# First block's output projection at 512 columns a product and tile by tile, and more points of giving way in the RWKV chain

## The chip, the core and the metric

The kernel runs on one core of one Trainium2 chip. The metric is the time of one execution on the device in microseconds, here the median of several runs; the trace is one execution taken by the hardware profiler. TensorE is PE in the rows (its weight loads PEld), VectorE is DVE, ScalarE ACT, GpSimd POOL; SP issues most of the DMA.

## The reference

Three blocks follow each other on one sequence of 1,024 tokens of width 1,024, in fp32. Cut to what the change touches:

```python
# first block: three mixers, gated and merged, then the output projection and a layer norm
log_om = where(causal, log_sigmoid(-z), 0)               # stick-breaking attention, blocks of 128 tokens
weights = masked_exp(causal, log_sigmoid(z) + reverse_cumsum(log_om) - log_om)
...
out = einsum('btd,de->bte', merged, w_out)               # 1024 x 1024 x 1024
x = layer_norm(DEEPNORM_ALPHA * x + out, ln_g, ln_b)

# second block: RMS norm, one wide projection, RWKV-7 time mix beside dilated attention
xn = rms_norm(h, norm_w)
p = einsum('bsd,dn->bsn', xn, w_in)
# time mix, per head of 64 and per token
sa = einsum('bhvk,bhk->bhv', state, av_t)
state = state * w_t + sa[..., None] * bv_t + v_t[..., None] * k_t
y_t = einsum('bhvk,bhk->bhv', state, r_t)
```

The third block follows and is not touched.

## The kernel before

Every fp32 operand of a dense product is split in a high and a low part (`split`: ACT casts the high part, DVE subtracts), and a product is three matmuls, high by high, high by low and low by high (`mm3`, L310 to L312). Dense products of the projections into a mixer keep 128 weight columns in the array and stream 512 tokens. Python generators write the program: `interleave` takes from each generator a count of expected steps and a start and an end in relative time, and always advances the one that is furthest behind by steps done over that count; each `yield` is a point where another may be written. What is written is then ordered by the scheduler of the recording layer for each engine; every engine executes its own instructions in that order.

*The mixes of the first block* (`mixing1`) run in six stages. In stage n the dense products of mixer n and some gates are interleaved with the mix of mixer n - 1. The stick-breaking mix (`stick`, stages two and three) goes over eight blocks of 128 tokens: products (L568), two sigmoids on ACT, masks and a reversed scan on DVE (L577), a multiply (L578), transposes on PE (L589), copies (L591) and products with the values (L597). `M1` gives `interleave` the count of its steps, 60, which is also how many there are.

*The output projection* is in `out1`. After the up projections (eight steps of L310 to L312 into `m`, twice) it holds the merged activations as `macts`, 128 x 512 in each of eight pieces for each half of the tokens. `wout(hf)` does one half of the tokens, four tiles of 128: for each quarter of 256 output columns `tok4_gen` streams the eight weight slices past the four tiles (L362 to L364, 256 columns a matmul) into two PSUM banks, and `ev` adds the residual x (L838) and takes statistics (L839). The x of a half is loaded ahead of it (L832). After the last quarter of a half `norms` finishes a tile: layer norm (L795 to L802; for the first `LNP` tiles one multiply on ACT and the addition on POOL, for the others one pass on DVE), the store of the result, and the RMS norm of the second block (`norm_act`, L860 to L862). `to_acts` transposes a normalized tile (L873) and splits it into `nacts`. The second half's products are interleaved with the transposes of the first half's tiles, and those of the second half with `rwkv_start`, four dense products of the second block on the first half of the tokens. Weights come through a pool of three raw buffers and five split ones.

*The RWKV time mix* (`rwkv`) has 16 units (pair of heads and half of the tokens), in 18 iterations. In iteration `it` it interleaves the chain of unit it - 2 (`rw_chain`), the inverse of unit it - 1 (`rw_inverse`, 62 small DVE passes), the features of unit it (`rw_feat`) and dense products (`rw_dense` and attention jobs). The chain has eight chunks of 64 tokens. Each is a line of dependent steps: products with the state (L1169), copies of the result into `R` on DVE and ACT (L1170, L1171), a product (L1174), copies into `SV` (L1175, L1176), a product (L1178), the new state on DVE (L1182) and a product into the output (L1183). A chunk has one `yield`, at its end. After the chunks the unit's output is normed (L1190 to L1197), transposed (L1204) and gated.

Of the kernel before, what the change touches and what calls it, by code (L numbers as in the profile page):

```python
# [10 lines left out]
F32R = mybir.dt.float32r  # L11
# [7 lines left out]
D = 1024  # L19
# [82 lines left out]
def layout(a):  # L102
# [41 lines left out]
    quarters = lambda w: f(w.reshape(-1, 128, w.shape[1] // 256, 256).transpose(2, 1, 0, 3))  # L144
    o["w1out"] = quarters(a["w_out"][0])
    o["w2out"] = quarters(a["w_out_2"])
# [4 lines left out]
    o["w3fm"] = tiles(w3, 8)  # L151
    halves = lambda w: f(w.reshape(-1, 128, w.shape[1] // 512, 512).transpose(2, 1, 0, 3))
    o["w3v"] = halves(w3[:, 512:1024])
# [27 lines left out]
MRB = 2  # L181
GNY = 4
TRM = (0.0, 0.8)
YD = 0
LNP = 4
HGD = 1
# [17 lines left out]
class Kern:  # L204
# [342 lines left out]
    def stick(self, pm, pr, q, k, v, y):  # L547

        nc = self.nc
        for i in range(NT):  # L550
# [10 lines left out]
            for h in range(2):  # L561
# [17 lines left out]
                bes.append(be)  # L579
                yield  # L580
            po = self.mm_ps()[:, :128]
            for g0 in range(0, i + 1, 4):
# [182 lines left out]
    def out1(self, acts):  # L765
# [4 lines left out]
        with self.weights(*WB[1]), tc.tile_pool(name="pu", bufs=1, reuse_waits="tile") as pu, self.psum(mx=4, tp=2):  # L770
# [22 lines left out]
            def norms(i, r, st):  # L793
                mv = self.t(pu, [128, 4], "lnmv", bufs=2)
                V.bn_aggr(mv[:, 0:2], st)  # L795
                self.rsqrt(pu, mv[:, 2:3], mv[:, 1:2], 1.0, 1e-5)
                V.scalar_tensor_tensor(r, r, mv[:, 0:1], g, ALU.subtract, ALU.mult)
                if i < LNP:
                    nc.scalar.activation(r, r, AF.Identity, scale=mv[:, 2:3])
                    nc.gpsimd.tensor_tensor(r, r, b, ALU.add)  # L800
                else:
                    V.scalar_tensor_tensor(r, r, mv[:, 2:3], b, ALU.mult, ALU.add)  # L802
                nc.scalar.dma_start(self.hd[i], r)
                return self.norm_act(pu, r, nw, 1e-5)

# [20 lines left out]

            def wout(hf):
                rs, sts = [], []
                for i in range(4):
                    rs.append(self.t(po, [128, D], "r", bufs=8))  # L830
                    sts.append(self.t(pu, [128, 4, 6], "lnst", bufs=8))
                    nc.sync.dma_start(rs[i], I["x"][512 * hf + 128 * i:512 * hf + 128 * i + 128])  # L832
                for q in range(4):

                    def ev(i, ps, q=q):
                        r, st = rs[i - 4 * hf], sts[i - 4 * hf]
                        qs = slice(256 * q, 256 * q + 256)
                        V.scalar_tensor_tensor(r[:, qs], r[:, qs], ALPHA, ps, ALU.mult, ALU.add)  # L838
                        V.bn_stats(st[:, q], r[:, qs])  # L839
                        if q == 3:  # L840
                            pend.append((i, norms(i, r, st)))
                    yield from self.tok4_gen(I["w1out"][q], macts, range(4 * hf, 4 * hf + 4), ev)

            def late():
                while pend:
                    self.to_acts(*pend.pop(0), nacts)
                    yield
            for _ in wout(0):
                pass
            interleave([(wout(1), 64, 0.0, 1.0), (late(), 4, 0.3, 0.9)])  # L850
            self.acts = nacts
            interleave([(self.rwkv_start(), 32, 0.0, 1.0), (late(), 4, 0.2, 1.1)])
            po_pool.__exit__(None, None, None)

    def norm_act(self, pool, h, nw, eps):

        nc = self.nc
        xs = self.t(pool, [128, D], "xs", bufs=2)
        ms = self.t(pool, [128, 2], "ms", bufs=2)
# [74 lines left out]
    def rwkv(self):  # L934
        nc, tc, I = self.nc, self.tc, self.I
        with tc.tile_pool(name="rw", bufs=1, reuse_waits="tile") as rw, self.psum(mx=2, iv=1, ch=1, cy=1):
# [15 lines left out]
            for it in range(18):  # L952
                gens = []
                if it >= 2:
                    gens.append((self.rw_chain(rw, U[it - 2]), 11 + GNY, *PLAN[0]))
                if 1 <= it <= 16:
                    gens.append((self.rw_inverse(rw, U[it - 1]), 37, *PLAN[1]))
                if it < 16:
                    gens.append((self.rw_feat(rw, U[it]), 20, *PLAN[2]))
                jobs = list(islice(att, ATT[it]))  # L960
# [22 lines left out]
    def rw_feat(self, rw, S):  # L983
# [20 lines left out]
        yield  # L1004
        V.tensor_tensor_scan(sg, self.c("cm"), sg, 0.0, ALU.mult, ALU.add)
        e1 = self.t(rw, [128, 8, 65], "E1")
        ei = ff("ei")
        nc.gpsimd.memset(e1[:, :, 0:1], 1.0)
        nc.scalar.activation(e1[:, :, 1:65], c8(sg), AF.Exp, scale=-cc)
        nc.scalar.activation(ei, sg, AF.Exp, scale=cc)  # L1010
        S["dc"] = dc = self.t(rw, [128, 8], "dc", bufs=3)
# [134 lines left out]
    def rw_chain(self, rw, S):  # L1146
# [16 lines left out]
        for c in range(8):  # L1163
# [8 lines left out]
            for n, s in enumerate((E, O)):  # L1172
                nc.scalar.activation(sd[s], sv[s, c, n], AF.Identity, scale=dc[s])  # L1173
            nc.tensor.matmul(up, xs[:, c], R, start=True, stop=True)  # L1174
            V.tensor_copy(sv[E, c, 0], up[E])  # L1175
            nc.scalar.copy(sv[O, c, 1], up[O])  # L1176
            both = sv[:, c].rearrange("p n v -> p (n v)")
            nc.tensor.matmul(sp, M3[:, c].rearrange("p n k -> p (n k)"), both, start=True, stop=True)  # L1178
            for n, s in enumerate((E, O)):
# [12 lines left out]
        TT(c8(y), c8(y), bc(st[:, 0:8]), ALU.add)  # L1192
        nc.scalar.activation(sq, y, AF.Square)
        yield
        V.tensor_reduce(st[:, 8:16], c8(sq), AX.X, ALU.add)
# [559 lines left out]
```

## Time and profile before

| | |
|---|---|
| median of 3 runs | 2845.41 us (2844.46 to 2849.97) |
| the profiled execution | 2842.42 us |
| its span | 2840.6 us |
| mean granted TensorE clock in it | 0.986 of full |
| busy: PE, PEld | 96%, 80% of the span |
| busy: DVE, ACT, POOL | 62%, 41%, 10% |

The span is the time from the first to the last instruction in the trace. The bars of matmuls overlap, so PE's busy share is how long it had something in work, not how much of its rate was used.

### The profile page before, as it was taken

How to read it: one execution, taken by the hardware profiler on the slowest of the kernel's cores; microseconds unless marked ns; L12 is line 12 of the kernel's file. 1: busy time of each engine (PE TensorE's matmuls, PEld its weight loads, DVE VectorE, ACT ScalarE, POOL GpSimd, SP SyncE). 2: the span in 40 equal slices, each digit the busy share in tenths (PEclk: the TensorE clock that was granted, in tenths of full speed). 3: DMA queues.
4: the chain of work that ended last, by engine and by line, in shares of the span. 5: the costliest groups of instructions: out<-in, count | busy, mean ns of one | idle time of the engine just before them, and what ended most of it. 6: DMA issues, size and time to landing. Idle time of an engine off the chain costs nothing. (4 is left out here: it accounts for less than half of the span.)

```text
span 2840.6 us, 50116 instructions
## 1 busy us (share of the span) xinstructions
PE 2732.7 (96%) x18984; PEld 2277.3 (80%) x18984; DVE 1762.3 (62%) x4655; ACT 1174.7 (41%) x2808; POOL 275.5 (10%) x370
## 2 busy tenths in 40 slices
PE   9999999999998999999999999989999999999999
PEld 7778787777798787778877778768889989978887
DVE  4665533433867567787787877765466676644354
ACT  4433323223324324444445444444465666442232
POOL 0000000000213100010011100100011211000100
PEclk9999999999999999999999999989999999999999
DMA  3121111114753322222222222222754553331132
GB/s 124 45 68 45 56 65 38 57 57 148 226 191 115 98 85 66 72 74 69 78 66 79 69 72 75 68 66 73 209 181 143 165 161 109 132 118 66 48 121 97
DMA packets 215265, 276.63 MB, mean 97 GB/s; under 512 B 70112, under 2 KB 105712, under 8 KB 214896
## 3 DMA queue, kind: packets, MB, share of 16 engines
q1 hardware_dynamic: 187024, 220.99, 25.4%
q10 hardware_dynamic: 28000, 52.44, 5.1%
q8 instruction: 149, 2.44, 0.4%
q14 instruction: 92, 0.75, 0.1%
HBM read 213.58 MB, written 59.77 MB: 96 GB/s over the span
## 5 line engine op out<-in xcount | busy, mean ns | idle before, releaser
L310 PE MATMUL pd<-aH,wh 128*128 128x512 f32 (+1 forms) x1824 | 758.5, 416 | 12.4 <-ACT aH L305 5.9
L312 PE MATMUL pd<-aH,wl 128*128 128x512 f32 (+1 forms) x1824 | 735.1, 403 | 2.2 <-DVE wl L282 2.2
L311 PE MATMUL pd<-aL,wh 128*128 128x512 f32 (+1 forms) x1824 | 731.2, 401 | 0.0
L282 DVE TENSOR_TENSOR wl<-wraw,wh 128x512 fp32r<-128x512 f32 (+1 forms) x429 | 305.0, 716 | 303.1 <-ACT wh L281 293.5
L281 ACT CAST wh<-wraw 128x512 fp32r<-128x512 f32 (+1 forms) x429 | 260.4, 611 | 433.8 <-PE pd L311 214.3
L310 PEld LDWEIGHTS pd<-aH,wh 128*128 128x128 f32 (+1 forms) x1824 | 345.8, 190 | 85.2 <-issue 14.4
L312 PEld LDWEIGHTS pd<-aH,wl 128*128 128x128 f32 (+1 forms) x1824 | 345.3, 189 | 72.6 <-DVE wl L282 4.5
L311 PEld LDWEIGHTS pd<-aL,wh 128*128 128x128 f32 (+1 forms) x1824 | 346.5, 190 | 57.9 <-DVE aL L306 0.4
L310 PE MATMUL pd<-wh,aH 128*128 128x256 f32 x960 | 283.1, 296 | 2.7 <-ACT wh L281 2.2
L311 PE MATMUL pd<-wl,aH 128*128 128x256 f32 x960 | 273.7, 286 | 0.9 <-DVE wl L282 0.9
L312 PE MATMUL pd<-wh,aL 128*128 128x256 f32 x960 | 272.1, 286 | 1.4 <-DVE aL L306 1.2
L310 PEld LDWEIGHTS pd<-wh,aH 128*128 128x128 f32 x960 | 183.4, 192 | 7.7 <-ACT wh L281 3.4
L311 PEld LDWEIGHTS pd<-wl,aH 128*128 128x128 f32 x960 | 183.8, 192 | 4.1 <-DVE wl L282 1.8
L312 PEld LDWEIGHTS pd<-wh,aL 128*128 128x128 f32 x960 | 183.3, 192 | 2.7 <-DVE aL L306 2.3
L1447 ACT ACTIVATE S<-S,anm 128x256 f32<-128x256 f32 (+1 forms) x256 | 118.0, 463 | 22.5 <-DVE anm L1440 19.5
L1173 ACT ACTIVATE sd<-SV,dc 64x64 f32<-64x64 f32 x256 | 88.4, 345 | 83.6 <-DVE SV L1182 78.4
L1111 DVE TENSOR_TENSOR Xt<-At,X 128x60 f32<-128x60 f32 (+24 forms) x496 | 106.4, 214 | 11.1
L1113 DVE TENSOR_TENSOR X<-X,Xt 128x60 f32<-128x60 f32 (+24 forms) x496 | 104.7, 211 | 12.2
L1398 DVE CUSTOM_DVE_ANT_0 S<-sc,cf 128x256 f32<-128x256 f32 (+1 forms) x256 | 86.1, 377 | 31.3 <-PE sc L1395 21.7
L1394 PE MATMUL sc<-kk,qq 128*128 128x256 f32 (+1 forms) x256 | 90.5, 369 | 4.6 <-DVE kk L1369 3.6
L1169 PEld LDWEIGHTS cy<-SV,M 128*128 128x128 f32 x512 | 81.1, 193 | 16.2 <-DVE SV L1182 4.1
L1182 DVE SCALAR_TENSOR_TENSOR SV<-ch,dc,sd 64x64 f32<-64x64 f32 x240 | 67.9, 283 | 30.6 <-PE ch L1178 24.2
(376 smaller groups left out, 4857.2 us busy)
## 6 DMA issues: line engine op xcount, KB each, us to landing
wraw<-in_w2fm SPq DMA_DIRECT2D x122, 256.0 KB, 2.7
wraw<-in_w1fm SPq DMA_DIRECT2D x80, 256.0 KB, 2.6
qkr<-qkg SPq DMA_DIRECT2D x152, 128.0 KB, 2.8
wraw<-in_w2out SPq DMA_DIRECT2D x64, 256.0 KB, 3.4
sgd<-s ACTq DMA_DIRECT2D x48, 256.0 KB, 2.0
sgt<-sgd SPq DMA_DIRECT2D x48, 256.0 KB, 3.6
qkg<-ast ACTq DMA_DIRECT2D x42, 256.0 KB, 2.0
wraw<-in_w3fm SPq DMA_DIRECT2D x38, 256.0 KB, 2.6
```

Source lines behind the costliest of these rows:

```text
L281: nc.scalar.copy(h, raw)
L282: nc.vector.tensor_tensor(l, raw, h.bitcast(F32), ALU.subtract)
L310: mm(ps, lh, rh, start=start, stop=False)
L311: mm(ps, lh, rl, start=False, stop=False)
L312: mm(ps, ll, rh, start=False, stop=stop)
L1111: eng.tensor_tensor(tmp[:, :M, :n], At[:, j:j + 1, j + 1:32].to_broadcast([128, M, n]), X[:, :M, j:j + 1].to_broadcast([128, M, n]), ALU.mult)
L1113: eng.tensor_tensor(X[:, :M, j + 1:32], X[:, :M, j + 1:32], tmp[:, :M, :n], ALU.add)
L1169: nc.tensor.matmul(xy[:, c, n], M1[:, c, n], sv[:, c, n], start=c % 4 == 0 and n == 0, stop=False, skip_group_check=True)
L1173: nc.scalar.activation(sd[s], sv[s, c, n], AF.Identity, scale=dc[s])
L1394: mm(o, q, k, start=i == 0, stop=False, skip_group_check=True)
L1398: red = lambda o, x, mk, acc: V.tensor_tensor_reduce(o, x, mk, 1.0, -3e38, ALU.add, ALU.max, acc)
L1447: nc.scalar.activation(x, x, AF.Exp, bias=nm[:, n, h, t:t + 1], accum_out=l[:, n, h, t:t + 1])
```

## The change

- `w1out` is packed in two halves of 512 columns in place of four quarters of 256.
- `wout` is gone. All eight tiles of x are loaded at once. The first 512 output columns are done for four tiles at a time, with the weight slices streamed past them; for the second four, two of the PSUM banks come from the dense pool. Then the weights of the second 512 columns are loaded and split once into a pool of their own, and `second` does one tile after the other with them: 24 matmuls, residual, statistics, norms. After five tiles the transposes of the first four are interleaved with the other three.
- `LNP` goes from 4 to 7, and the buffers of `xs` from 2 to 4.
- `stick` yields 1 + i // 3 more times ahead of the transposes of block i, so a mix has 75 steps; `M1` still says 60.
- In `rw_chain` each chunk has three yields in place of one, there is one more after the square, and `GNY` goes from 4 to 8; its count follows (30 + GNY). In `rw_feat` the scan and the two exponentials are done in halves with yields behind them; its count goes from 20 to 22.

```diff
-GNY = 4
+GNY = 8
...
-LNP = 4
+LNP = 7
...
@@ stick
                 bes.append(be)
                 yield
+            for _ in range(1 + i // 3):
+                yield
...
@@ out1
-                return self.norm_act(pu, r, nw, 1e-5)
+                return self.norm_act(pu, r, nw, 1e-5, 4)
...
+            rs = [self.t(po, [128, D], f"r{i}") for i in range(NT)]
+            sts = [self.t(pu, [128, 2, 6], f"lnst{i}") for i in range(NT)]
+            for i in range(NT):
+                nc.sync.dma_start(rs[i], I["x"][128 * i:128 * i + 128])
+            half = lambda n: slice(512 * n, 512 * n + 512)
+            def products(i, k, ps, w):
+                sl = slice(128 * (i % 4), 128 * (i % 4) + 128)
+                self.mm3(ps, macts[0][i // 4][:, k, sl], macts[1][i // 4][:, k, sl], *w, k == 0, k == 7)
+            def add(i, n, ps):
+                V.scalar_tensor_tensor(rs[i][:, half(n)], rs[i][:, half(n)], ALPHA, ps, ALU.mult, ALU.add)
+                V.bn_stats(sts[i][:, n], rs[i][:, half(n)])
+            for t0 in (0, 4):
+                ps = [self.dn_ps() if t0 and j < 2 else self.mm_ps() for j in range(4)]
+                for k, w in enumerate(self.w_slices(I["w1out"][0], [128, 8, 512])):
+                    for j in range(4):
+                        products(t0 + j, k, ps[j], w)
+                for j in range(4):
+                    add(t0 + j, 0, ps[j])
+            def second():
+                ws = [self.t(pw, [128, 8, 512], "wo" + x, F32R) for x in "HL"]
+                for k in range(8):
+                    raw = self.t(self.wp, [128, 512], "wraw", bufs=self.wr)
+                    nc.sync.dma_start(raw, I["w1out"][1][:, k])
+                    self.split(ws[0][:, k], ws[1][:, k], raw)
+                for i in range(NT):
+                    ps = self.mm_ps()
+                    for k in range(8):
+                        products(i, k, ps, (ws[0][:, k], ws[1][:, k]))
+                    add(i, 1, ps)
+                    pend.append((i, norms(i, rs[i], sts[i])))
+                    yield
-            for _ in wout(0):
+            s = second()
+            for _ in range(5):
+                next(s)
+            interleave([(s, 4, 0.0, 1.0), (late(4), 4, 0.0, 0.9)])
+            for _ in late(4):
                 pass
-            interleave([(wout(1), 64, 0.0, 1.0), (late(), 4, 0.3, 0.9)])
...
@@ rw_feat
-        V.tensor_tensor_scan(sg, self.c("cm"), sg, 0.0, ALU.mult, ALU.add)
...
-        nc.scalar.activation(e1[:, :, 1:65], c8(sg), AF.Exp, scale=-cc)
-        nc.scalar.activation(ei, sg, AF.Exp, scale=cc)
+        halves = [(slice(256 * n, 256 * n + 256), slice(4 * n, 4 * n + 4)) for n in range(2)]
+        for tk, cs in halves:
+            V.tensor_tensor_scan(sg[:, tk], self.c("cm")[:, 0:256], sg[:, tk], 0.0, ALU.mult, ALU.add)
+            yield
+        for tk, cs in halves:
+            nc.scalar.activation(e1[:, cs, 1:65], c8(sg)[:, cs], AF.Exp, scale=-cc)
+            nc.scalar.activation(ei[:, tk], sg[:, tk], AF.Exp, scale=cc)
+            yield
...
@@ rw_chain
                 nc.scalar.activation(sd[s], sv[s, c, n], AF.Identity, scale=dc[s])
+            yield
             nc.tensor.matmul(up, xs[:, c], R, start=True, stop=True)
...
             both = sv[:, c].rearrange("p n v -> p (n v)")
+            yield
             nc.tensor.matmul(sp, M3[:, c].rearrange("p n k -> p (n k)"), both, start=True, stop=True)
```

How the instructions stand now. On PE, the start of the output projection before: `mx` is the PSUM tile, `wh` and `wl` the weight slice that streams, `aH` and `aL` the activations.

```order
L362 MATMUL mx_7925<-wh_7927,aH_1092_7111 128x256
L363 MATMUL mx_7925<-wl_7928,aH_1092_7111 128x256
L364 MATMUL mx_7925<-wh_7927,aL_1093_7112 128x256
L362 MATMUL mx_7925<-wh_7927,aH_1092_7111 128x256
L363 MATMUL mx_7925<-wl_7928,aH_1092_7111 128x256
L364 MATMUL mx_7925<-wh_7927,aL_1093_7112 128x256
```

And now, with four PSUM tiles a slice:

```order
L310 MATMUL mx_7937<-wh_7941,aH_1092_7111 128x512
L311 MATMUL mx_7937<-wl_7942,aH_1092_7111 128x512
L312 MATMUL mx_7937<-wh_7941,aL_1093_7112 128x512
L310 MATMUL mx_7938<-wh_7941,aH_1092_7111 128x512
L311 MATMUL mx_7938<-wl_7942,aH_1092_7111 128x512
L312 MATMUL mx_7938<-wh_7941,aL_1093_7112 128x512
L310 MATMUL mx_7939<-wh_7941,aH_1092_7111 128x512
```

The same three matmuls with twice the columns, and one PSUM bank for each tile in place of half a bank.

On SP, the queue of loads at the same place before: `wraw` from `w1out` are weight slices, `r` are tiles of x.

```order
L280 DMA wraw_8059<-in_w1out 128x512
L832 DMA r_7913<-in_x 128x1024
L832 DMA r_7916<-in_x 128x1024
L832 DMA r_7919<-in_x 128x1024
L832 DMA r_7922<-in_x 128x1024
L280 DMA wraw_8089<-in_w1out 128x512
L280 DMA wraw_8119<-in_w1out 128x512
L280 DMA wraw_8149<-in_w1out 128x512
L832 DMA r_8501<-in_x 128x1024
```

And now:

```order
L280 DMA wraw_8015<-in_w1out 128x512
L832 DMA r_1343_7913<-in_x 128x1024
L832 DMA r_1344_7914<-in_x 128x1024
L832 DMA r_1345_7915<-in_x 128x1024
L832 DMA r_1346_7916<-in_x 128x1024
L832 DMA r_1347_7917<-in_x 128x1024
L832 DMA r_1348_7918<-in_x 128x1024
L832 DMA r_1349_7919<-in_x 128x1024
L832 DMA r_1350_7920<-in_x 128x1024
L280 DMA wraw_8033<-in_w1out 128x512
L280 DMA wraw_8051<-in_w1out 128x512
```

Eight loads of x stand between the fifth and the sixth weight slice, where four stood.

On PE, the fifth chunk of the seventh unit of the RWKV chain before: `cy` is written with the state, `ch` from `R` and then from `SV`; the `pd` rows are dense products that stand between.

```order
L1169 MATMUL cy_14599<-SV_1574_9415,M_2288_13606 128x64 x2
L310 MATMUL pd_14912<-aH_1096_7115,wh_14900 128x512
L311 MATMUL pd_14912<-aL_1097_7116,wh_14900 128x512
L312 MATMUL pd_14912<-aH_1096_7115,wl_14901 128x512
L310 MATMUL pd_14912<-aH_1096_7115,wh_14900 128x512
L1174 MATMUL ch_14832<-R_14835,XS_1572_9413 128x64
L311 MATMUL pd_14912<-aL_1097_7116,wh_14900 128x512
L312 MATMUL pd_14912<-aH_1096_7115,wl_14901 128x512
L310 MATMUL pd_14912<-aH_1096_7115,wh_14900 128x512
L311 MATMUL pd_14912<-aL_1097_7116,wh_14900 128x512
L1178 MATMUL ch_14833<-SV_1574_9415,M_2326_13866 128x128
```

And the same chunk now (L1203, L1209 and L1214 are the old L1169, L1174 and L1178):

```order
L1203 MATMUL cy_14152<-SV_1536_8944,M_2262_13225 128x64
L311 MATMUL pd_14427<-aL_1097_7116,wh_14415 128x512
L312 MATMUL pd_14427<-aH_1096_7115,wl_14416 128x512
L310 MATMUL pd_14427<-aH_1096_7115,wh_14415 128x512
L311 MATMUL pd_14427<-aL_1097_7116,wh_14415 128x512
L312 MATMUL pd_14427<-aH_1096_7115,wl_14416 128x512
L1209 MATMUL ch_14388<-R_14391,XS_1534_8942 128x64
L310 MATMUL pd_14427<-aH_1096_7115,wh_14415 128x512
L311 MATMUL pd_14427<-aL_1097_7116,wh_14415 128x512
L312 MATMUL pd_14427<-aH_1096_7115,wl_14416 128x512
L310 MATMUL pd_14427<-aH_1096_7115,wh_14415 128x512
L1214 MATMUL ch_14389<-SV_1536_8944,M_2288_13431 128x128
```

More dense matmuls stand ahead of the second product here, and four, as before, ahead of the third.

## Rows read from the trace of the kernel before

**Rows 1.** The page, part 1: busy time of each engine over the whole span.

```profile
PE 2732.7 (96%) x18984; PEld 2277.3 (80%) x18984; DVE 1762.3 (62%) x4655; ACT 1174.7 (41%) x2808; POOL 275.5 (10%) x370
```

**Rows 2.** Timeline of PE, 919 to 940: start us, us, instruction [idle before, releaser].

```profile
919.50 0.76 PE L310 MATMUL pd<-aH,wh 128*128 128x512 f32 x1 [2.41 <-DVE lo L903]
...
933.19 0.39 PE L311 MATMUL pd<-aL,wh 128*128 128x512 f32 x1
933.42 0.39 PE L312 MATMUL pd<-aH,wl 128*128 128x512 f32 x1
935.42 0.65 PE L1101 MATMUL iv<-cf,rkv 128*128 128x128 f32 x4 [1.61 <-DVE rkv L903]
938.18 0.50 PE L310 MATMUL pd<-aH,wh 128*128 128x512 f32 x1 [2.11 <-ACT wh L281]
```

**Rows 3.** Timeline of PE around 855.

```profile
855.11 0.28 PE L364 MATMUL mx<-wh,aL 128*128 128x256 f32 x1
855.23 0.28 PE L362 MATMUL mx<-wh,aH 128*128 128x256 f32 x1
859.38 0.58 PE L362 MATMUL mx<-wh,aH 128*128 128x256 f32 x1 [3.87 <-DVE r L838]
```

**Rows 4.** Source view of L362: duration ns min/median/max, first and last start.

```profile
L362 PE MATMUL mx<-wh,aH x256: 277/283/583, 795.4 to 900.3; 128*128 128x256 f32 x128
```

**Rows 5.** Windows, two stretches: engines' busy us, PEclk, DMA share, GB/s.

```profile
860.00:864.00 4.00, 4.00 (x20) 4.00 (x20) 3.03 (x7) 1.66 (x2) 2.92 (x3) 0.50 0.52 197
1860.00:1990.00 130.00, 117.28 (x776) 98.46 (x777) 75.62 (x268) 53.93 (x145) 7.55 (x8) 0.91 0.21 65
```

**Rows 6.** Lines of 1020 to 1990: busy us, mean ns, idle before, releasers.

```profile
L1174 PE MATMUL ch<-R,XS 128*128 128x64 f32 x256 | 50.3, 278 | 19.6 <-ACT R L1171 17.6 <-ACT XS L1140 0.8
L1178 PE MATMUL ch<-SV,M 128*128 128x128 f32 x256 | 56.1, 301 | 3.0 <-ACT SV L1176 2.3
L1204 PE MATMUL ch<-cf,tt 128*128 128x128 f32 x60 | 10.1, 289 | 7.9 <-DVE tt L1197 7.8
```

**Rows 7.** Timeline of one chunk of the RWKV chain, at 1475.

```profile
1475.02 0.60 PE L1169 MATMUL cy<-SV,M 128*128 128x64 f32 x4
...
1475.97 0.21 ACT L1171 COPY R<-cy 64x64 f32<-64x64 f32 x1 [0.42 <-DVE R L1170]
...
1476.23 0.43 PE L1174 MATMUL ch<-R,XS 128*128 128x64 f32 x2
```

**Rows 8.** Lines of 60 to 335, the stick-breaking transposes on PE.

```profile
L589 PE MATMUL mx<-cf,be 128*128 128x128 f32 x144 | 24.4, 278 | 10.7 <-DVE be L578 10.7
```

**Rows 9.** Timeline of PE, the last block of the second stick-breaking mix.

```profile
303.26 0.73 PE L568 MATMUL mx<-f,q 128*128 128x512 f32 x2
...
315.62 0.82 PE L589 MATMUL mx<-cf,be 128*128 128x128 f32 x6
```

**Rows 10.** Lines of 795 to 930 on POOL.

```profile
L800 POOL TENSOR_TENSOR r<-r,br_ln_b 128x1024 f32<-128x1024 f32 x4 | 11.9, 2982 | 2.1 <-ACT r L799 2.1
L732 POOL TENSOR_TENSOR lnmv<-lnmv,mhalf 128x1 f32<-128x1 f32 x8 | 10.2, 1275 | 75.4 <-DVE lnmv L731 75.4
L732 POOL TENSOR_TENSOR ms<-ms,mhalf 128x1 f32<-128x1 f32 x8 | 5.7, 708 | 18.5 <-DVE ms L731 17.0 <-DVE lnmv L731 1.5
```

**Rows 11.** Timeline around 848, POOL and DVE.

```profile
847.95 3.21 POOL L800 TENSOR_TENSOR r<-r,br_ln_b 128x1024 f32<-128x1024 f32 x1 [1.26 <-ACT r L799]
...
849.32 2.93 DVE L797 SCALAR_TENSOR_TENSOR r<-r,lnmv,br_ln_g 128x1024 f32<-128x1024 f32 x1
```

**Rows 12.** Source view of L797: duration ns min/median/max.

```profile
L797 DVE SCALAR_TENSOR_TENSOR r<-r,lnmv,br_ln_g x8: 1274/1276/3012, 845.0 to 914.0; 128x1024 f32<-128x1024 f32 x8
```

**Rows 13.** Source view of L832: first and last start, time to landing.

```profile
L832 SPq DMA_DIRECT2D r<-in_x x8: 382/456/1062, 796.1 to 814.6; - x8
...
DMA to landing us min/median/max: 5.3/6.3/7.6
```

**Rows 14.** Source view of L1197: once in each unit, first and last start.

```profile
L1197 DVE TENSOR_TENSOR tt<-tt,gst x16: 691/693/1094, 1116.8 to 1990.3; 128x512 f32<-128x512 f32 x16
```

More of the change, by code (lines that the diff above doesn't have):

```diff
@@ L144, in layout @@
     quarters = lambda w: f(w.reshape(-1, 128, w.shape[1] // 256, 256).transpose(2, 1, 0, 3))
-    o["w1out"] = quarters(a["w_out"][0])
+    halves = lambda w: f(w.reshape(-1, 128, w.shape[1] // 512, 512).transpose(2, 1, 0, 3))
+    o["w1out"] = halves(a["w_out"][0])
     o["w2out"] = quarters(a["w_out_2"])
@@ L151, in layout @@
     o["w3fm"] = tiles(w3, 8)
-    halves = lambda w: f(w.reshape(-1, 128, w.shape[1] // 512, 512).transpose(2, 1, 0, 3))
     o["w3v"] = halves(w3[:, 512:1024])
@@ L825, in out1 @@
             pend = []
[L827 to L842, printed above, removed]
@@ L844, in late @@
-            def late():
-                while pend:
+            rs = [self.t(po, [128, D], f"r{i}") for i in range(NT)]
[6 more added lines that the diff above has]
+                self.mm3(ps, macts[0][i // 4][:, k, sl], macts[1][i // 4][:, k, sl], *w, k == 0, k == 7)
@@ L846, in late @@
+            def late(n):
+                while pend and pend[0][0] < n:
                     self.to_acts(*pend.pop(0), nacts)
                     yield
-            for _ in wout(0):
+            pw_pool = tc.tile_pool(name="pw", bufs=1, reuse_waits="tile")
+            pw = pw_pool.__enter__()
+            s = second()
[3 more added lines that the diff above has]
+            for _ in late(4):
                 pass
-            interleave([(wout(1), 64, 0.0, 1.0), (late(), 4, 0.3, 0.9)])
+            pw_pool.__exit__(None, None, None)
@@ L851, in out1, with norm_act @@
             self.acts = nacts
-            interleave([(self.rwkv_start(), 32, 0.0, 1.0), (late(), 4, 0.2, 1.1)])
+            interleave([(self.rwkv_start(), 32, 0.0, 1.0), (late(NT), 4, 0.2, 1.1)])
             po_pool.__exit__(None, None, None)
-    def norm_act(self, pool, h, nw, eps):
+    def norm_act(self, pool, h, nw, eps, bufs=2):
         nc = self.nc
-        xs = self.t(pool, [128, D], "xs", bufs=2)
+        xs = self.t(pool, [128, D], "xs", bufs=bufs)
         ms = self.t(pool, [128, 2], "ms", bufs=2)
@@ L954, in rwkv @@
                 if it >= 2:
[L955 removed]
+                    gens.append((self.rw_chain(rw, U[it - 2]), 30 + GNY, *PLAN[0]))
                 if 1 <= it <= 16:
@@ L958, in rwkv @@
                 if it < 16:
-                    gens.append((self.rw_feat(rw, U[it]), 20, *PLAN[2]))
+                    gens.append((self.rw_feat(rw, U[it]), 22, *PLAN[2]))
                 jobs = list(islice(att, ATT[it]))
@@ L1193, in rw_chain @@
         nc.scalar.activation(sq, y, AF.Square)
+        yield
         yield
```

## The prediction

> **What bounds the kernel now.** I read the page first: PE is busy for 96% of the span [rows 1]. That busy time is not its pace, because a matmul's bar of 0.39 us is longer than the 0.23 us after which the next one starts [rows 2]. So I take the start-to-start time as the price: 0.23 us for 512 columns [rows 2] and 0.12 us for 256 [rows 3]. At these paces PE has work almost throughout, and no other engine is near its limit; the span can shrink only by fewer paces of PE or by the places where PE stands. The change touches three stretches, and I read each by its waits.
>
> *The output projection and what follows it.* It starts at 795.4 us [rows 4], and the four dense products of `rwkv_start` behind it end just before L1101 at 935.4 [rows 2]: 140.0 us. The work in it is 768 matmuls of 256 columns (92.2 us), 96 of 512 (22.1) and 64 transposes (7.0, at 0.11 us, an estimate from L1101's four in 0.65 us, of which the last bar is some 0.3 [rows 2]): 121.3. So 18.7 us are lost there, and 2.1 more behind L1101 [rows 2]. The longest piece stands at 855: a 3.9 us wait for DVE's evacuation [rows 3], which is queued behind the norms of the first four tiles. After it the granted clock is 0.50, the lower of its two levels (1.2 GHz), through 860 to 864 [rows 5].
>
> *The RWKV chain.* PE stands before the chain's matmuls for 19.6 us (L1174), 3.0 (L1178) and 7.9 (the transposes L1204): 30.5 us of 970 [rows 6]. One chunk shows why: the matmuls L1169 begin at 1475.02, R is ready 1.16 us later when ACT's copy ends (1475.97 + 0.21), and L1174 starts 0.05 us behind that [rows 7]. Five matmuls of 512 columns, 1.15 us, are needed to cover that way. In 1860 to 1990, where dense work runs out, the mean clock is 0.91 [rows 5].
>
> *The stick-breaking mix* loses 10.7 us before its transposes, all to the DVE chain of scan and multiply [rows 8].
>
> **The output projection, step by step.** 768 matmuls at 0.12 become 384 at 0.23: 92.2 to 88.3 us, a gain of 3.9. Of 32 weight slices 24 are left, each split on ACT and DVE; both are off the path here, so I count nothing for the eight.
>
> Of the 20.8 us of stalls, I expect the change to remove the 3.9 us wait with its slow clock (4 us at half pace, 2 us lost), and most waits of the late transposes. The reason is that the norms now come one tile at a time. A tile is 24 x 0.23 = 5.5 us of PE. POOL needs 2.98 + 1.28 + 0.71 = 5.0 us for each [rows 10], as seven tiles now go through its add instead of four. DVE needs two passes of 1,024 (1.27 each undisturbed [rows 12]) and two of 512; these lie between 0.64 and 1.27, and I take 0.8: 4.2 us and some short ones. Both stay under 5.5, so tile 0 is normalized long before its transposes, which stand after the sixth tile's products; the others follow at PE's pace.
>
> Three more tiles go through POOL's add, and the rows show its price: an L797 that ran while the add was going (847.95 to 851.16) took 2.93 us [rows 11] and not 1.27; the longest was 3.01 [rows 12]. These two over four adds make 0.85 us a tile, and DVE's 4.2 become 5.1, still under 5.5. The Trainium skill, "Perfetto Trace Analysis", section "Optimizing Scalar/DVE Operations", says that GpSimd and VectorE share a read port to SBUF, so that work offloaded between the two may gain nothing. By that rule the trace's slow passes are no accident. If each add held DVE for its whole 2.98 us, a tile would cost 7.2 there, 1.7 over PE's 5.5: 13 us late after eight tiles, of which the 22 us of `rwkv_start` hide about half; that is part of the second rival.
>
> New waits: eight loads of x (4 MB) now stand ahead of the sixth weight slice in SP's order; before it was four. Those four landed 5.3 to 7.6 us after issue [rows 13]. Five slices cover 5 x 12 x 0.23 = 13.8 us, so the sixth is wanted at 809. If 2 MB need 7 to 9 us from 796.1 [rows 13], 4 MB need 13 to 19 and the slice lands at 810 to 816: a wait of 0 to 7 us; I take 3, with 2 for the clock after it. PE is in order, so all of the projection stands behind it. What stays as it was: a dense product that waits for an evacuation (2.4 us at 919.5) and the 1.6 + 2.1 us around L1101 [rows 2]. In all 11 us instead of 20.8: 10 gained, so **-14 us** with the pace. Bounds: -21 if only the last pair stays, +3 if the load wait is 7, the norms come late and each costs a slow clock.
>
> **The RWKV chain.** No work is added but a few instructions (scan and two exponentials cut in halves). The yields move other work between a chunk's steps. From the orders of both kernels I counted, for all 128 chunks, the matmuls between L1169's and L1174's by their paces: chunks with under 1.2 us fall from 84 to 47, and between L1174 and L1178 from 83 to 58, so 44% and 30% fewer uncovered steps. The place is taken from the gap between units, of which some 11 us at these paces are left to cover the norm. I take 40% of 30.5 us: **-12 us**. Bounds: nothing (the same DVE queue is moved along with it), and the whole 30 plus 12 us, if the slow clock of 1860 to 1990 goes as well (0.09 x 130 us x 2 at half pace, half of it lost).
>
> The cost is on the chain itself: on the mean 0.25 + 0.22 us more stand in a chunk, 4 us a unit. A unit lasts 58 us (L1197, once in each [rows 14]), and 24 steps like the 1.2 us of rows 7 take 29, so this costs nothing while dense products fill the rest; only in the last three units is that cover thin.
>
> **The stick-breaking mix.** One to three yields come before the transposes, with the count given to `interleave` left at 60 where 75 now come. In the order the matmuls before the transposes grow from some 3.2 us to 4 to 6, so most of the 10.7 us goes; I take 9. But the mix now ends after the dense work of its stage: its last block has 26 dense matmuls (6.0 us) and 2.4 us of its own between its first products and last transposes, which were 12.3 us apart [rows 9]. 3.9 us open, twice: 8. Net **-1 us**, bounds -10 and +12 (a slow clock behind both).
>
> **Sum.** The profiled execution took 2842.4 us (its span 2840.6), 3.0 under the median of the three runs shown. 2842.4 - 14 - 12 - 1 = 2815.4, and against that median **2818 us**.
>
> **Rivals.**
> - *The chain's stalls only move.* Order is not time: DVE's copy of R waits behind the same DVE passes, now later ones. For it: PE's waits are for ACT and DVE copies, not for matmuls. Against it: R came 1.16 us after L1169 whatever PE did. Then 2842.4 - 15 + 3 = 2830. Chance 0.20.
> - *The projection gives nothing back*: the loads' wait 7, the norms some 6 late, 4 for two slow clocks, so +3 where I have -14: 2835. For it the long L797 [rows 12]; against it POOL's 5.0 below 5.5. Chance 0.10.
> - *The change does not do what it says*: the first two together, or a new stall of their size: within 0.2% of before. Chance 0.09. (0.2% is about 6 us, what a measurement of this kernel can just tell from no change.)
> - *More comes back*: PE's whole 30.5 and the clock of 1860 to 1990: 2842.4 - 14 - 30 - 12 + 3 = 2789. Chance 0.05.
> - *Slower, by the chain in the last three units.* There it is the path, with little dense work to cover it. Each of three yields per chunk may let a DVE pass of 0.7 us (L1197's size [rows 14]) in front of the next copy: 2.1 us x 24 chunks = 50 us, a net of +23: 2868. It decides from 27 / 24 = 1.1 us per chunk. Against it: in that stretch the order puts no more DVE passes between the copies than before. Chance 0.09.
>
> **How the numbers follow.** The likeliest case, all three terms near their values, has 0.47 and spans 2800 to 2828. The range 2787 to 2843 adds the first two rivals and the fourth, and reaches into the unchanged case; what is left out holds 0.2. Faster by over 0.2%: 0.47 + 0.20 + 0.10 + 0.05 = 0.82; within: 0.09; slower: 0.09.
>
> **What would show it.** In the projection: L310 to L312 at 0.23 us a start, no 3.9 us wait for an evacuation, a wait for a weight slice some 14 us after the start, and L1135 (the old L1101) at some 126 us after the projection's start, not 140. In RWKV: waits before L1209 and L1214 lower by 40%, and units below 58 us. In the mix: no 1 us waits before L591 except at the end of the second and third stages. I am wrong if waits before L1209 are as long as before, if tile norms come later than their transposes, or if the stretch from the last dense unit to the attention takes longer than the 130 us of 1860 to 1990.

## The result

The changed kernel takes 2812.20 us (median of 4 runs, 2807.45 to 2816.09) against 2847.69 (4 runs, 2844.46 to 2849.99): ratio 0.9874, interval [0.9857, 0.9891], so 31 to 41 us less. I had forecast 2818, 27 us less.

The execution that was profiled took 2816.09 us, the slowest of the four, with a span of 2814.3 us, 26.3 under that of before; the table adds up to that and not to the medians. It cuts the span at four first starts: the projection's first product (before L362, now L310 from `macts`), the transposes of rkv (L1101, now L1135), the chain's first product (L1169, now L1203) and attention's first (L1394, now L1431).

| stretch | before | after | difference |
|---|---|---|---|
| to the projection's first product | 795.4 | 788.2 | -7.2 |
| projection to the transposes of rkv | 140.0 | 131.4 | -8.6 |
| from there to the chain's first product | 135.8 | 137.4 | +1.6 |
| chain to the attention | 949.3 | 935.6 | -13.7 |
| attention to the last matmul | 812.9 | 814.5 | +1.6 |

All three places gave something, not in the sizes of my sum (projection -14, chain -12, mix -1).

**The mix.** Lines of the stretch 60 to 335 after, the row that answers to [rows 8]:

```profile
L591 PE MATMUL mx<-cf,be 128*128 128x128 f32 x144 | 22.8, 277 | 4.6 <-DVE be L578 4.6
```

10.7 us of waits became 4.6. The loss was larger than "idle" says: idle is counted from the end of the modelled bar (0.39 us), while the next start was due after 0.23. Start to start, 12 waits of before (the 11 of that row and one of 1.0 us before L597) took 16.7 us where 2.8 would do, the 5 of after 6.5 where 1.2 would: 8.6 us back. The timeline of PE in the last block of the second mix, which answers to [rows 9]:

```profile
303.23 0.94 PE L568 MATMUL mx<-f,q 128*128 128x512 f32 x3
...
310.65 0.41 PE L591 MATMUL mx<-cf,be 128*128 128x128 f32 x2 [1.13 <-DVE be L578]
...
315.35 0.88 PE L591 MATMUL mx<-cf,be 128*128 128x128 f32 x6 [0.61 <-DVE be L578]
```

From the first products to the transposes at 315 12.1 us pass, 12.4 before; 1.7 of them PE waits, not 3.9. (The last transposes of this block come only at 318; the prediction's 12.3 us end at the same place as these.)

**The projection.** Lines of 836 to 905 on PE, the second half and the first dense products behind it:

```profile
L902 PE MATMUL tp<-cf,xs 128*128 128x128 f32 x48 | 7.1, 286 | 4.9 <-DVE aL L306 4.9
```

It is one wait, at 873.76 to 879.07: the second pair of tile transposes needs the PSUM of the first, whose cast (L305) and subtract (L306) come late. ACT shows why (timeline; L801 scales a tile, L805 stores it, L889 squares it, L305 is the cast):

```profile
870.66 1.06 ACT L889 ACTIVATE xs<-r 128x1024 f32<-128x1024 f32 x1 [3.74 <-POOL r L802]
871.62 0.18 ACT L889 ACTIVATION_READ_ACCUMULATOR xs<-r 128x1 f32 x1
871.78 1.15 ACT L801 ACTIVATE r<-r,lnmv 128x1024 f32<-128x1024 f32 x1
876.24 0.33 ACTq L805 DMA_DIRECT2D hd<-r  x1
876.67 1.06 ACT L889 ACTIVATE xs<-r 128x1024 f32<-128x1024 f32 x1 [3.74 <-POOL r L802]
877.63 0.19 ACT L889 ACTIVATION_READ_ACCUMULATOR xs<-r 128x1 f32 x1
877.73 1.05 ACT L305 CAST aH<-tp 128x512 fp32r<-128x512 f32 x2
```

and POOL beside it:

```profile
873.01 3.20 POOL L802 TENSOR_TENSOR r<-r,br_ln_b 128x1024 f32<-128x1024 f32 x1 [0.32 <-ACT r L801]
```

ACT's square of a tile waits for POOL's add; the scaling of the next tile stands behind that square; the next add waits for the scaling. From 870.66 it is 1.12 us to the scaling, 1.23 to the add, 3.20 of add and 0.46 to the next square: a ring of 6.0 us a tile, of which POOL works 5.3 and ACT 2.7. The tile's products need 5.5. The add itself is not of one length (source view of L802; ns, min/median/max):

```profile
L802 POOL TENSOR_TENSOR r<-r,br_ln_b x7: 2375/3186/3263, 849.9 to 891.2; 128x1024 f32<-128x1024 f32 x7
```

At its shortest, 2.4 us, the ring would be 5.2 (an estimate), under 5.5.

The wait that I had put at the sixth weight slice does not show, but only because PE came late itself. The loads of x (source view of L832, answering to [rows 13]) and of the three weight slices behind them (source view of L280, 793 to 797.5):

```profile
L832 SPq DMA_DIRECT2D r<-in_x x8: 377/449/632, 788.9 to 792.6; - x8
...
DMA to landing us min/median/max: 4.4/8.0/10.7
```

```profile
L280 SPq DMA_DIRECT2D wraw<-in_w1out x3: 327/328/328, 793.4 to 796.9; - x3
...
DMA to landing us min/median/max: 8.3/9.3/10.6
```

The sixth slice is the first of these three: it landed 10.6 us after its issue, at 803.9, and its cast began 0.1 us behind that (timeline of ACT):

```profile
804.03 1.87 ACT L281 CAST wh<-wraw 128x512 fp32r<-128x512 f32 x3 [8.95 <-PE mx L312]
```

The row names PE, but the wait was for the load: the casts that the profile puts down to a load start 0.1 us behind a landing too, and in the run without the add, below, it names the load. PE came to the slice at 806.57, 18.4 us after its first product and not 13.8, for it had waited 2.6 us for `m` at the start, with the clock at 0.50 from 793.5 to 796.9 (timeline of PE):

```profile
789.79 0.50 PE L310 MATMUL mx<-wh,aH 128*128 128x512 f32 x1 [0.78 <-DVE m L820]
793.28 0.65 PE L310 MATMUL mx<-wh,aH 128*128 128x512 f32 x1 [1.83 <-DVE m L820]
```

Without these it would have come at 802.0, 2.7 us ahead of the cast's end (an estimate). In the run without the add, with a full clock there, PE did wait for that cast (timelines of ACT and PE):

```profile
806.69 1.27 ACT L281 CAST wh<-wraw 128x512 fp32r<-128x512 f32 x2 [9.67 <-DMA wraw<-in_w1out]
```

```profile
807.36 0.50 PE L310 MATMUL mx<-wh,aH 128*128 128x512 f32 x1 [0.27 <-ACT wh L281]
```

**The chain.** Lines of 1000 to 1990, answering to [rows 6]:

```profile
L1203 PE MATMUL cy<-SV,M 128*128 128x64 f32 x512 | 83.5, 270 | 6.4 <-DVE SV L1218 5.9
...
L1214 PE MATMUL ch<-SV,M 128*128 128x128 f32 x256 | 56.0, 301 | 4.3 <-ACT SV L1211 3.9
...
L1209 PE MATMUL ch<-R,XS 128*128 128x64 f32 x256 | 48.9, 273 | 9.6 <-ACT R L1205 6.8 <-ACT tt L1245 2.4
L1241 PE MATMUL ch<-cf,tt 128*128 128x128 f32 x64 | 10.4, 284 | 3.4 <-DVE tt L1234 3.4
```

For the first of these the row before (lines of 1020 to 1990) is:

```profile
L1169 PE MATMUL cy<-SV,M 128*128 128x64 f32 x512 | 79.6, 264 | 1.8 <-ACT tt L1189 1.3 <-DVE SV L1182 0.2
```

The wait for R halved (19.6 to 9.6) and that of the norm's transposes too (7.9 to 3.4); the waits for the state (1.8 to 6.4) and for SV (3.0 to 4.3) grew.

### The profile page after: what moved, and what is told of

Same layout as the page of the kernel before. It is cut to its first block, busy times and chain, and to the rows that moved or that the text cites. A ratio compares the mean times of both kernels' runs of the same rounds, so it can differ in the third digit from the quotient of the medians.

```text
span 2814.3 us, 49316 instructions
## 1 busy us (share of the span) xinstructions
PE 2721.6 (97%) x18600; PEld 2257.7 (80%) x18600; DVE 1740.6 (62%) x4628; ACT 1177.2 (42%) x2835; POOL 283.8 (10%) x373
## 4 chain that ended last, share of the span: by engine, by line
PE 45%; DVE 6%; issue 3%; ACT 2%; DMA 2%; POOL 1%; SPq 0%; ACTq 0%; POOLq 0%; DVEq 0%
PE pd L310 8%; PE pd L311 8%; PE pd L312 8%; PE po L1509 2%; PE mx L1100 2%; PE mx L310 2%; PE mx L312 2%; PE mx L311 2%; PE tr L1519 1%; PE sc L1431 1%; PE sc L1432 1%; PE cy L1203 1%; PE ch L1214 1%; DVE wl L282 1%; DMA wraw<-in_w2out 1%
## 5 line engine op out<-in xcount | busy, mean ns | idle before, releaser
L310 PE MATMUL pd<-aH,wh 128*128 128x512 f32 (+1 forms) x1824 | 760.7, 417 | 10.2 <-ACT aH L305 6.1
L282 DVE TENSOR_TENSOR wl<-wraw,wh 128x512 fp32r<-128x512 f32 (+1 forms) x413 | 291.8, 713 | 283.0 <-ACT wh L281 273.0
L281 ACT CAST wh<-wraw 128x512 fp32r<-128x512 f32 (+1 forms) x413 | 250.2, 611 | 382.1 <-PE pd L311 193.1
L310 PEld LDWEIGHTS pd<-aH,wh 128*128 128x128 f32 (+1 forms) x1824 | 345.6, 190 | 74.2 <-ACT aH L305 6.4
L310 PE MATMUL pd<-wh,aH 128*128 128x256 f32 (+1 forms) x976 | 288.7, 297 | 3.6 <-ACT wh L281 3.1
L311 PE MATMUL pd<-wl,aH 128*128 128x256 f32 (+1 forms) x976 | 278.6, 287 | 2.3 <-DVE wl L282 2.1
L312 PE MATMUL pd<-wh,aL 128*128 128x256 f32 (+1 forms) x976 | 276.8, 286 | 1.1 <-DVE aL L306 0.9
L310 PEld LDWEIGHTS pd<-wh,aH 128*128 128x128 f32 x976 | 186.0, 191 | 7.5 <-ACT wh L281 4.4
L1203 PEld LDWEIGHTS cy<-SV,M 128*128 128x128 f32 x512 | 80.2, 191 | 29.0 <-DVE SV L1218 17.7
L1431 PE MATMUL sc<-kk,qq 128*128 128x256 f32 (+1 forms) x256 | 91.1, 371 | 4.3 <-DVE kk L1406 3.3
L1203 PE MATMUL cy<-SV,M 128*128 128x64 f32 x512 | 83.5, 270 | 6.4 <-DVE SV L1218 5.9
```

The source lines that it names most:

```text
L281: nc.scalar.copy(h, raw)
L282: nc.vector.tensor_tensor(l, raw, h.bitcast(F32), ALU.subtract)
L310: mm(ps, lh, rh, start=start, stop=False)
L311: mm(ps, lh, rl, start=False, stop=False)
L312: mm(ps, ll, rh, start=False, stop=stop)
L1203: nc.tensor.matmul(xy[:, c, n], M1[:, c, n], sv[:, c, n], start=c % 4 == 0 and n == 0, stop=False, skip_group_check=True)
```

## Experiments

Each was timed in five rounds against the kernel before on the same chip; differences are the ratio's, with its interval, in us.

### The three parts alone

Each run is the kernel before with one part of the change.

> Only the output projection's part of the change, the rest as before. By the trace after, the stretch from the projection's first product to the transposes of rkv takes 131.4 us instead of 140.0, and a slow clock behind it costs 1 to 2: -7 to -9 us against before. By the term of the prediction, -14. By the rival that the projection gives nothing back, 0 to +3. The 4.9 us wait before the second group of tile transposes should be there without the other two parts as well.

Measured: ratio 0.9964 [0.9949, 0.9978], -10 us [-14, -6]. From the projection's first product to the transposes of rkv 129.6 us; the wait before the second pair of transposes is there (4.5 us).

> Only the RWKV part (yields in the chunks, GNY 8, the halved scan and exponentials). By the trace after, from the first L1203 to the attention 935.6 us instead of 949.3: -12 to -14 us. By the term of the prediction, -12. By the rival that the chain's stalls only move, 0 (waits before the second and third product then as long as before, or as much more before L1203).

Measured: 0.9957 [0.9941, 0.9972], -12 us [-17, -8]; chain to attention 936.2 us. The rival that the stalls only move is out for the part as a whole.

> Only the points of giving way of the stick-breaking mix. By the trace after, twelve waits of about 1 us become five and one short slow clock comes in: -5 us. By the term of the prediction, where the tail of two stages opens, -1 (waits of 3.9 us at the end of both stages).

Measured: 0.9969 [0.9957, 0.9981], -9 us [-12, -5]; waits of 4.6 us before L591, the projection's first product at 788.8. My -1 lies outside the interval. The traces of all runs agree: in the six whose mix is as before the projection's first product comes at 795.4 to 800.4, in the eight with the new one at 784.4 to 790.1.

The three add up to -31 where the whole gives -36 [-41, -31]: the 5 us between lie within the intervals of the parts, so nothing shows that the parts help or hinder each other.

### Does the mix's tail cost 8 us?

```diff
-M1 = [60, 60, 46, 46, 78]
+M1 = [75, 75, 46, 46, 78]
```

> The changed kernel with the count of the two stick-breaking stages at their true 75 steps, not 60. By the prediction's step (3.9 us open at the end of two stages) 8 us less than the changed kernel: about -43 against before. By the trace after, where the ends of the stages hold 3.8 us of waits and a short slow clock: at most -4, so -35 to -39. Rival: at 75 fewer dense products stand before each block's transposes and the waits of 1 us come back: -28 to -34.

Measured: 0.9876 [0.9861, 0.9891], -35 us [-40, -31], as the changed kernel. The waits before L591 did fall further (lines of 60 to 335):

```profile
L591 PE MATMUL mx<-cf,be 128*128 128x128 f32 x144 | 22.9, 276 | 1.3 <-ACT om L570 1.1 <-DVE be L578 0.2
```

but these 3.3 us, less a new wait of 1.0 before L599, are too few to tell in the time. There were no 8 us.

### What holds the projection's end

```diff
                 if i < LNP:
                     nc.scalar.activation(r, r, AF.Identity, scale=mv[:, 2:3])
-                    nc.gpsimd.tensor_tensor(r, r, b, ALU.add)
```

> The changed kernel without GpSimd's add in the norm of the first seven tiles: the bias ln_b is left out of them. Theory: a ring of GpSimd's add (3.2 us), ScalarE's square of that tile and its scaling of the next (1.1 + 1.15, in order on ScalarE) sets 6.0 us a tile, more than the 5.5 us of its products, and the casts of tile 0 queue behind it. Without the add the ring falls below 5.5, the 4.9 us wait and its slow clock go: 5 to 8 us less than the changed kernel, -40 to -43 against before. Rival: the place is only the first of several, and what is saved is waited for again before the products and transposes of rwkv_start: -33 to -36 against before, as the changed kernel.

Measured: 0.9894 [0.9874, 0.9913], -30 us [-36, -25]. The rival holds. Without the add the wait before the transposes went, and came back at the first dense products of `rwkv_start` (lines of 836 to 905):

```profile
L311 PE MATMUL pd<-aL,wh 128*128 128x512 f32 x14 | 6.3, 453 | 3.4 <-DVE aL L306 3.4
L901 PE MATMUL tp<-cf,xs 128*128 128x128 f32 x45 | 6.3, 274 | 0.8 <-DVE aL L306 0.8
L310 PE MATMUL pd<-aH,wh 128*128 128x512 f32 x14 | 6.1, 445 | 1.6 <-ACT aH L305 1.6
```

5.8 us instead of 5.4 at the same three places, and 131.1 us for the stretch against 131.4. Taking the add out took the first wait away; the ring was not what bounds the stretch.

Two runs of the changed kernel move the add of some tiles to VectorE (`LNP = 4`, and `if i % 2 == 0` in place of `if i < LNP`).

> The changed kernel with LNP 4: tiles 4 to 6 scale and add their bias in one VectorE pass, not by ScalarE and GpSimd. Ring theory: the casts of tile 0 no longer queue behind GpSimd's add of tile 4, so the 4.9 us wait falls under 2, but VectorE gets three more passes of 1.28 us and the last evacuations come later: -38 to -32 us against before, about the changed kernel's -35. Rival, that VectorE is the tighter engine in this stretch: the waits before the products of rwkv_start grow by these 3.8 us and a slow clock: -31 to -27.

> The changed kernel with GpSimd's add on the even tiles only and VectorE's one pass on the odd ones, so that no two tiles in a row are in the ring of GpSimd and ScalarE. Ring theory: under 5.5 us a tile on the mean, the 4.9 us wait falls under 2: -37 to -40 us against before if nothing else is late, -33 to -36 if it is waited for again at the products of rwkv_start, as without the add.

Measured: LNP 4 0.9899 [0.9886, 0.9912], -29 us [-33, -25], 138.1 us for the stretch; alternating 0.9905 [0.9892, 0.9918], -27 us [-31, -23], 137.8. Both cost some 6.5 us there, and the second lies outside both of its expectations. The first wait did not fall under 2 us as the ring theory had said: it is 4.6 us with LNP 4 and 3.9 alternating, and later waits grew. In all PE stands idle 4.6 and 2.7 us longer in the stretch, and the mean granted clock there is 0.95 and 0.94, 0.97 in the changed kernel. Extra passes on VectorE hurt, as the rival of the first said. So I formed the theory of two holds, ring and VectorE's sum, and took both away:

```diff
-                V.bn_stats(sts[i][:, n], rs[i][:, half(n)])
+                if n == 0:
+                    V.bn_stats(sts[i][:, n], rs[i][:, half(n)])
...
-                    pend.append((i, norms(i, rs[i], sts[i])))
+                    pend.append((i, norms(i, rs[i], sts[i][:, 0:1])))
```

> The changed kernel without GpSimd's add (the bias is left out of the first seven tiles) and without the statistics of the second half of each row (mean and variance come from 512 columns). Theory: two things hold the last evacuations, GpSimd's ring of 6.0 us a tile and VectorE's own 6.2 us a tile (4.8 of norm and 1.4 of subtracting the transposed halves) against 5.5 us of products, and each alone is enough. With both under 5.5 the waits between the sixth tile and the first products of rwkv_start (5.8 us in the run without the add) fall under 2: -38 to -43 us against before. Rival: it is the order on the engines (evacuations queued behind norms of later tiles), not the sum: no gain again, -28 to -35.

> The changed kernel without the statistics of the second half of each row alone (mean and variance from 512 columns); GpSimd's add stays. Theory of two holds: the ring still sets 6.0 us a tile, so the 4.9 us wait stays: -33 to -37 us against before, as the changed kernel. Rival, that VectorE's sum alone is the hold: -38 to -43.

Measured: both 0.9885 [0.9866, 0.9904], -33 us [-38, -27], 129.7 us; statistics alone 0.9895 [0.988, 0.991], -30 us [-34, -26], 135.0. Neither is faster than the changed kernel, and the theory of two holds falls. With both taken away one wait of any length is left, at the first dense product (timeline of PE):

```profile
888.54 0.80 PE L311 MATMUL pd<-aL,wh 128*128 128x512 f32 x1 [3.91 <-DVE aL L306]
```

and DVE shows it is the order (timeline; L839 adds the last tile's products, L799, L803 and L891 are its norm and the scaling of the tile before, L306 the subtract that PE waits for):

```profile
882.83 0.69 DVE L839 SCALAR_TENSOR_TENSOR r<-r,mx 128x512 f32<-128x512 f32 x1 [2.12 <-PE mx L312]
883.55 1.28 DVE L799 SCALAR_TENSOR_TENSOR r<-r,lnmv,br_ln_g 128x1024 f32<-128x1024 f32 x1
...
884.87 1.28 DVE L803 SCALAR_TENSOR_TENSOR r<-r,lnmv,br_ln_b 128x1024 f32<-128x1024 f32 x1
886.60 1.28 DVE L891 SCALAR_TENSOR_TENSOR xs<-r,ms,br_norm_w 128x1024 f32<-128x1024 f32 x1 [0.44 <-POOL ms L734]
887.80 1.28 DVE L306 TENSOR_TENSOR aL<-tp,aH 128x512 fp32r<-128x512 f32 x2
```

DVE is idle for 2.1 us waiting for the last tile's products, then does that tile's norm, and only then the subtracts of tile 3, which the dense products need. The statistics alone took 3.6 us more in that stretch than the changed kernel: the waits from the tile transposes to the first dense products are 7.0 us, not 5.4 (the first of them 2.6, where the theory kept 4.9), and the clock is at 0.50 for 10.2 us, not 6.8, which at half pace is 1.7 more. Why these waits grew stays open, and an order with the subtracts ahead of the last tile was not tried.

### Which piece of the RWKV part gives it

The kernel before with the halved scan and exponentials alone, with the chunk's yields alone, and with the yields and GNY 8:

```diff
-                    gens.append((self.rw_chain(rw, U[it - 2]), 11 + GNY, *PLAN[0]))
+                    gens.append((self.rw_chain(rw, U[it - 2]), 27 + GNY, *PLAN[0]))
...
+            yield
             nc.tensor.matmul(up, xs[:, c], R, start=True, stop=True)
...
+            yield
             nc.tensor.matmul(sp, M3[:, c].rearrange("p n k -> p (n k)"), both, start=True, stop=True)
```

> The kernel before with the halved scan and exponentials alone (count 22). Theory of the prediction: they shorten only the rare copy that stands behind a long scan: 0 to -3 us. Rival: -8 to -12.

> The kernel before with the two points of giving way inside each chunk alone (count 27 + GNY to match; GNY 4, whole scans). Theory of the prediction: covering the copies of R and of SV by dense products is what the RWKV part gives, so -8 to -12 us, with the waits before the second product at about half of 19.6 us. Rival: the halved scan and exponentials, which stand on VectorE and ScalarE ahead of these copies, give it: 0 to -4.

> The kernel before with the two points of giving way in each chunk (as in the run that took 25 us more) and GNY 8 instead of 4; scan and exponentials whole. Theory: by the proportional interleaving the 16 new steps took the share of time from the norm's steps at a unit's end (4 of 31 steps, not 4 of 15), so that its transposes waited (24.6 us, not 7.9) and the state came late (14.1, not 1.8); GNY 8 gives the share back: -10 to -13 us, as the whole RWKV part. Rival: the chunk's points of giving way cost by themselves and only the halved passes pay for them: +10 to +25.

Measured: halves 1.0002 [0.9991, 1.0012], no change; chunk's yields 1.0088 [1.0072, 1.0104], 25 us slower; yields with GNY 8 1.0049 [1.0033, 1.0064], 14 us slower. For the second run theory and rival both fall; for the third the rival holds: the yields cost by themselves. Between its +14 and the -12 of the whole part stand the halved passes, worth nothing alone, the late yield behind the square and a count of 38 in place of 35; these were not run apart. Lines of 1020 to 2060, yields alone:

```profile
L1169 PE MATMUL cy<-SV,M 128*128 128x64 f32 x512 | 81.1, 271 | 14.1 <-DVE SV L1184 13.5 <-ACT tt L1191 0.4
...
L1175 PE MATMUL ch<-R,XS 128*128 128x64 f32 x256 | 49.0, 274 | 10.0 <-ACT R L1171 6.7 <-ACT tt L1210 2.7
L1206 PE MATMUL ch<-cf,tt 128*128 128x128 f32 x64 | 10.7, 292 | 26.0 <-DVE tt L1199 18.9 <-DVE X L1113 3.7 <-DVE Xt L1111 3.4
```

and yields with GNY 8:

```profile
L1169 PE MATMUL cy<-SV,M 128*128 128x64 f32 x512 | 81.4, 269 | 2.7 <-DVE SV L1184 2.2 <-ACT tt L1191 0.3
...
L1175 PE MATMUL ch<-R,XS 128*128 128x64 f32 x256 | 49.1, 274 | 27.0 <-ACT R L1171 24.5 <-ACT tt L1210 2.4
L1206 PE MATMUL ch<-cf,tt 128*128 128x128 f32 x64 | 10.4, 286 | 9.5 <-DVE tt L1199 9.5
```

GNY does what I expected: the norm's transposes (L1206) wait 9.5 instead of 26.0, since 4 of 31 steps had been too small a share of a unit. But the wait for R, which the yields had halved, is back and longer. So in these two runs the stalls do only move, and grow; the mean granted clock of the stretch from the chain to the attention, 0.97 in both and 0.99 before, adds to that. Most of what moves is one thing. Before, the waits for R are not spread over 128 chunks: 12 of them, once in most units, hold 15.4 of the 19.6 us, and in each the instruction ahead of R's copy on ACT is one of the two exponentials of the features (L1009, L1010). One, in the timeline of DVE before:

```profile
1452.45 1.22 DVE L1005 TENSOR_TENSOR_SCAN fs<-cf,fs 128x512 f32<-128x512 f32 x1
```

of ACT:

```profile
1453.70 0.63 ACT L1009 ACTIVATE E<-fs 128x512 f32<-128x512 f32 x1 [1.68 <-DVE fs L1005]
1454.35 0.21 ACT L1171 COPY R<-cy 64x64 f32<-64x64 f32 x1
```

and of PE:

```profile
1454.61 0.43 PE L1174 MATMUL ch<-R,XS 128*128 128x64 f32 x2 [1.45 <-ACT R L1171]
```

The scan takes 1.22 us of DVE, its exponential stands on ACT, and R's copy behind both. With the yields alone the scan lands ahead of the state's update instead (timelines of DVE and PE of that run; in 10 of its 13 waits of over 0.3 us before L1169 the scan is the instruction ahead of the update):

```profile
1459.67 1.22 DVE L1005 TENSOR_TENSOR_SCAN fs<-cf,fs 128x512 f32<-128x512 f32 x1
1460.80 0.57 DVE L1184 SCALAR_TENSOR_TENSOR SV<-ch,dc,sd 64x64 f32<-64x64 f32 x2
```

```profile
1461.11 0.76 PE L1169 MATMUL cy<-SV,M 128*128 128x64 f32 x4 [1.66 <-DVE SV L1184]
```

With GNY 8 scan and exponentials are ahead of R again: in 5 of that run's 23 waits of over 0.3 us the second exponential is the instruction ahead of R's copy on ACT, in 8 a square of the features (L1016, 0.72 us) that follows the exponentials there; these 13 hold 18.1 of the 27.0 us. In the changed kernel scans are 0.69 us, and only two long waits for R (1.1 us each) stand behind an exponential. With halves alone 11 waits behind an exponential remain, 13.3 us; that too little dense work covers a step there is my reading and was not tested. The whole account rests on the traces of five kernels; the late yield and the count may have a share.

## Why the prediction was right or wrong

**The time** (2818 for 2812.2) is right, and so is the case: all three parts gain, and by the time all five rivals are out. That it came so close owes something to luck: the gain of 27 us that I forecast lies below the measured 31 to 41, and alone the projection gave 4 us less than its term and the mix 8 more, which partly cancels. Of the three terms one came out for another reason than mine, and two were mis-sized.

**Projection, -14, measured -10 [-14, -6].** The pace and the vanished 3.9 us wait came as worked out. The step "11 us instead of 20.8" failed: 16.1 are left (131.4 less 117.4 of work, and 2.1 behind it). It put 3 us and a slow clock at the sixth slice. The loads came as reckoned (the slice landed 15 us after the first load of x was issued, in my 13 to 19), but PE came 4.6 us later than I had reckoned, by waits for `m` and a slow clock there, which I had put at nothing: the loss stands at those. And it put nothing at the tile transposes and behind them, where 5.4 us stand and a slow clock. I had compared each engine's work per tile with 5.5 us, one engine at a time. The ring over two of them takes 6.0, and the work that evacuates the transposes, two casts and two subtracts a tile, was left out of the sum and stands in order behind later tiles' norms. The second rival came nearest, though late evacuations stood where it had late norms. It had DVE held by the add as the cause; the trace shows the ring, in which the add is the longest step, and DVE held in part. Source view of L799 after:

```profile
L799 DVE SCALAR_TENSOR_TENSOR r<-r,lnmv,br_ln_g x8: 1273/1639/3492, 847.0 to 893.4; 128x1024 f32<-128x1024 f32 x8
```

and without POOL's add:

```profile
L799 DVE SCALAR_TENSOR_TENSOR r<-r,lnmv,br_ln_g x8: 1274/1276/1280, 847.0 to 887.8; 128x1024 f32<-128x1024 f32 x8
```

An add beside it costs the median pass 0.36 us, the worst 2.2. That agrees in its sign with the rule of the Trainium skill, "Perfetto Trace Analysis", section "Optimizing Scalar/DVE Operations", that GpSimd and VectorE share a read port; but the add is not worth taking back to VectorE, where its tiles cost 6.5 us more.

**Chain, -12, measured -12 [-17, -8].** The size held by luck, for the reason did not. I counted chunks whose dense matmuls fall short of 1.2 us and took 40%; the loss was one long pass a unit in a queue ahead of a short copy, which no count of matmuls on PE shows. Of the waits summed over the four lines 32.3 became 23.7 us, 8.6 of the 13.7 by which the stretch shrank; the wait before L1214, which I expected 40% lower, grew. My sentence that the place "is taken from the gap between units" was the important one: with GNY 4 the yields alone cost 25 us, 14 with GNY 8. So the first rival, that stalls only move, is right of the yields alone. And I gave the slower rival, which looked only at the last three units, the wrong place: of the loss with GNY 4, 17.7 us come in the first 12 of 16 units, by the starts of L1169.

**Mix, -1, measured -9 [-12, -5].** The term that failed is the tail, "3.9 us open, twice". Start to start, the waits away from the ends of the two mixes cost 10.4 us less than before, for the 9 that I took. At the ends PE loses 4.5 us (waits of 1.1 and 1.0, then 1.1 and 0.6), not 8, and 2.7 of these it lost there before: a net cost of 1.8, and 8.6 in all. The 12 us from first products to transposes held; what I had wrong is the work that covers them. I counted 26 dense matmuls and 2.4 us besides; the trace has 30 and 3.2 us, 0.8 of these products with the values of the block before. Setting the count right gave no 8 us.

## What to carry to other kernels

Before costing a wait by the mean work that covers it, list the waits by time: once-a-unit waits name a long instruction in a queue ahead of a short one, and cutting it helped here only together with points of giving way that let other work in between. A forecast wait that does not show may be covered by another ahead of it, and can come back when that one goes. Check in-order rings across engines, not only each engine's sum against the period. And when a step count in a proportional interleaving grows, the other steps' share shrinks, so change the counts together.

## What was not expected of the hardware

The granted clock fell while PE was busy throughout. Windows of the changed kernel at the end of the second mix (engines' busy us, PEclk, DMA share, GB/s):

```profile
318.00:322.00 4.00, 4.00 (x85) 3.77 (x87) 2.97 (x7) 0.17 (x1) 0.10 (x1) 1.00 0.20 66
322.00:326.00 4.00, 4.00 (x36) 2.96 (x33) 2.79 (x9) 0.00 (x0) 0.00 (x0) 0.57 0.49 186
```

PE's last wait was 0.6 us at 315.35. From 317 to 324 it had run only short matmuls (128x2, 64x32 and 128x128 forms), and the clock was near the lower of its two levels (1.2 GHz of 2.4) until 326. Before, in the same place, a like run of short matmuls did not bring it down. But it is not the change: in the run with the RWKV part alone, whose mix is that of before, the clock fell in the same place too (window of that run):

```profile
323.00:327.00 4.00, 4.00 (x56) 3.07 (x53) 2.79 (x9) 0.00 (x0) 0.00 (x0) 0.57 0.32 131
```

and in the run with the mix's part alone it stayed at 1.00 from 318 to 330. So such a fall is not a cost of the new order, and what brings it down in one execution and not in another no run here shows.
